# Output projection: the recurrent half ahead of the memory attention, and the attentions traced later

## The chip, the cores and the metric

One Trainium2 chip, one of its cores. The kernel is one launch of one layer of a decoder trunk, batch 1, 256 tokens, model width 1024, all in float32. The metric is the device time in microseconds (us) of that launch. The layer's weights (about 84 MB) are read from HBM once.

## What is computed

```
x = x + 0.5 * swiglu(rms_norm(x, ffn1_norm), ffn1_w_in, ffn1_w_out)
u = rms_norm(x, mix_norm) @ w_in                     # 1024 -> 2048 columns
lru_x, lru_g, mq, mk, mv, cq = split(u)              # 512, 512, 256, 256, 256, 256
y_lru  = rg_lru(causal_conv4(lru_x)) * gelu(lru_g)   # recurrent half, 512 columns
y_moba = causal self-attention(mq, mk, mv)           # 4 heads x 64, ALiBi, QK norm
y_mem  = attention(cq, keys and values of rms_norm(mem) @ mem_w_kv)   # 4 heads x 64
x = x + concat(y_lru, y_moba, y_mem) @ w_out         # rows 0:512, 512:768, 768:1024
x = x + 0.5 * swiglu(rms_norm(x, ffn2_norm), ffn2_w_in, ffn2_w_out)
```

With 256 tokens there is one block of 256, so the block selection of the self-attention reduces to causal attention.

## The kernel before

**Products.** Every weight is split into a high part (`whi`) and a low part (`wlo`), every activation too, and a product is three TensorE (PE) matmuls: high times high, low weight times high, high weight times low. One such matmul has 128 rows and 512 columns. Tokens come in two tiles, t = 0 and 1.

**The stream.** All weights form one list, `stream`, of steps. A step is one half of a 1 MB unit: `halve` makes `whi` on ScalarE (ACT, line 119) and `wlo` on VectorE (DVE, line 121), three steps ahead, and `consume` traces the products of the step, 12 matmuls. Units are loaded by DMAs that SP issues, up to three units ahead (`raw`, 3 buffers); the halves have 7 buffers. Counted from `marks["kv"]`, steps 0 to 3 are the memory's keys and values, 4 to 7 the recurrent input (`use_x`), 8 to 11 queries and keys of the self-attention (`use_qk`), 12 to 15 its values and the memory's queries (`use_vc`), 16 to 19 the gate branch with its GeLU (`use_g`), 20 to 27 the output projection, and from 28 on the second FFN.

**Work beside the products.** `at(name, fn)` traces a piece of the mixer when the stream has come to step `PLAN[name]`. The pieces are the recurrence (`lru0` to `lru5`, lines 538 to 577), the transposes of the normed heads (`qkT`, `cT`; line 460, copied out of PSUM in lines 463 and 465), the scores of the self-attention (`moba_s`, line 606, softmax in 581 to 597), the scores of the memory attention (`mem_s`, line 619), the two `attend` (`moba_y`, `mem_y`; transposes of the probabilities in line 633, copies `pT` in lines 636 to 639, values in line 643, normed rows turned in line 652, split into parts in lines 150 and 151), and the turn of the recurrent output (`out0`, `out1`, line 704). The order of the trace is what the scheduler starts from; the order it settles on is fixed per engine, and each engine takes its instructions one after another.

**PSUM.** `ps_h` has 2 buffers (the products `h`), `ps_t` 2 (transposes), `ps_o` 4 (FFN outputs, gate products, scores, `y` of both attentions, and the four accumulators `o` of the projection).

**Heads' norm.** `heads_T` squares on ACT (line 449), sums on DVE (451), takes the power on GpSimd (POOL, lines 156 and 157), scales on DVE (454). The scaled rows `hsq` are what line 460 transposes.

**Projection.** `out_att` takes `yb` (self-attention) at steps 20 and 21 and `yc` (memory attention) at steps 22 and 23. `out_lru` holds four halves and at step 27 multiplies `ya` (recurrent half) by all four, tile by tile, adds the residual and transposes for the second FFN.

Of the kernel before, what the change touches and what calls it, by code (L numbers as in the profile page):

```python
# [8 lines left out]
F32 = mybir.dt.float32  # L9
# [6 lines left out]
P = 128  # L16
# [7 lines left out]
HD = 64  # L24
# [10 lines left out]
# steps after the memory's product at which the mixer's parts are traced  # L35
PLAN = dict(mk0=7, mkT0=7, mk1=6, mkT1=5, lxT0=8, lxT1=9, conv0=8, conv1=8, conv2=9, conv3=9, gate_a=10, gate_x=10,
            lru0=13, lru1=14, lru2=15, lru3=15, lru4=18, lru5=19, qkT0=11, qkT1=11, moba_s0=11, moba_s1=11, moba_y=17,
            cT0=15, cT1=15, mem_s0=15, mem_s1=15, mem_y=17, out0=21, out1=21)
WIDE = (0, 0, 0, 0, 0)
ORDER = (0, 2, 1, 3)  # heads in the order of the score tiles: two heads of one row tile share a PSUM bank  # L40
# [5 lines left out]
def hymba_layer(ctx, tc, x, mem, ffn1_norm, ffn1_w_in, ffn1_w_out, mix_norm, mem_norm, w_in,  # L46
# [22 lines left out]
    @contextmanager  # L69
    def in_order():  # L70
        """Each engine takes what is traced here in the order of the trace."""
        traced = nc.cur_bb.bb.instructions
        at = len(traced)
        yield
        last = {}
        for i in traced[at:]:
            if i.engine in last:
                tc.add_manual_dep(i, last[i.engine], mybir.DependencyInfo(
                    mybir.DependencyClass.NoSync, mybir.DependencyReason.DATA), reason="in_order")
            last[i.engine] = i.name  # L80

# [16 lines left out]
    class Unit:  # L98
# [3 lines left out]
        def load(self, part=None):  # L102
            """loads(raw): the DMAs' (tile, DRAM rows), in the order of the k tiles."""
# [8 lines left out]
        def halve(self, i, ways=1, pool_ways=()):  # L112
            """The i-th half's high and low parts, in steps: yields after each of the ways."""
# [16 lines left out]
    def in_unit(w, c0s, width, k0, single=False):  # L130
        """Four k tiles of w's columns [c0, c0 + width) for the given c0s: [P, 4, 512]."""
# [11 lines left out]
    def out_unit(w, r0):  # L143
        """Two k tiles of whole rows: [P, 2, 1024]."""
        wv = w[0, r0:r0 + 2 * P, :].rearrange("(k p) n -> p k n", p=P)
        return Unit(2, lambda raw: [(raw.rearrange("p (k n) -> p k n", k=2), wv)])

# [5 lines left out]
    def rsqrt(ss, n, count, out):  # L153
        """out = (ss / count + eps) ** -0.5, [P, n], on GpSimd."""
# [4 lines left out]
    def row_scale(a, name):  # L159
        """rsqrt(mean(a * a) + eps) over the row, [P, 1]."""  # L160
# [7 lines left out]
    def transposed(a, g, t, pre, src_pool=None):  # L168
        """(a * g) with the features on partitions, in two float32r parts."""
        return finish(transposed_steps(a, g, t, pre, src_pool))  # L170

    def transposed_steps(a, g, t, pre, src_pool=None):
        """Each half's transposes, scalings, high parts and low parts: yields after each of the eight."""
# [24 lines left out]
    stream = []  # L198

    def project(units, xT, use, wide=False):  # L200
        """h[t] = x[t] @ the two units' columns; then use(t, h)."""
# [128 lines left out]
    def later(fn, *args):  # L330
        """Traces fn's instructions behind all that was traced so far on each engine."""
# [6 lines left out]
    def parameters():  # L338
# [39 lines left out]
        # softplus(-lam) = max(-lam, 0) + 2 atanh(e / (2 + e)), e = exp(-|lam|)  # L378
# [26 lines left out]
        # ALiBi and the causal mask: the block on the diagonal, and the one below it  # L405
# [38 lines left out]
    def heads_T(name, src, n, dsts):  # L444
        """src [P tokens, n * HD]: RMS norm over each head, then dims on partitions."""
# [92 lines left out]
    def rate():  # L538
        """2 sigmoid(z) = exp(min(z, 0)) * (1 + |tanh(z / 2)|), right to the last bits for small ones too."""
# [5 lines left out]
    def decay():  # L545
        """th = tanh(s / 2), a = exp(-s) = (1 - th) / (1 + th), 1 - a^2 = 4 th / (1 + th)^2."""
# [7 lines left out]
    def decay2():  # L554
        """One Newton step from (1 + exp(-s)) / 2 towards 1 / (1 + th)."""
# [25 lines left out]
    def softmax_rows(s, w, from_psum):  # L581
        """exp(s - max) / sum over the last axis: [P, NH, w], heads in the order ORDER."""
# [30 lines left out]
    def mem_scores(t):  # L613
        ss = []
        for i in range(2):
            s = ps_o.tile([P, 2, SEQ], F32, name="s", tag="o")
# [6 lines left out]
    def attend(pr, v, causal, name):  # L623
        """y transposed: [P (two heads' dims), pair, tokens], in two parts."""
        pr, v = L[pr], L[v]
        wk = L["wk"]
        ys = [ps_o.tile([P, NH, HD], F32, name="y", tag="o") for _ in range(NT)]
# [54 lines left out]
    # the GeLU branch  # L682
# [48 lines left out]
    def out_lru(k):  # L731
        def go(u):
            held.append(u)
            if k < 3:
                return
            for t in range(NT):
                x2[t] = resp.tile([P, D], F32, name=f"xd{t}", tag="res")
                for hf in range(2):
                    for i in range(4):
                        out_rows(L["ya"], i, t, (hf,), held[i], False, i == 3)  # L740
# [7 lines left out]
    for r0, fns in ((512, [out_att("yb", k, True) for k in range(2)]), (768, [out_att("yc", k, False) for k in range(2)]),  # L748
                    (0, [out_lru(0), out_lru(1)]), (256, [out_lru(2), out_lru(3)])):
# [20 lines left out]
    def load_ahead(i):  # L770
        """Loads as many units as there is room for, when the halves before i are split."""
# [80 lines left out]
```

## Time and profile before

| | |
|---|---|
| time, median of 3 runs | 502.61 us (502.40 to 502.68) |
| span of the profiled execution | 501.6 us |
| PE busy | 485.5 us, 97% of the span |
| PE weight loads busy | 396.1 us, 79% |
| DVE busy | 314.8 us, 63% |
| ACT busy | 256.5 us, 51% |
| POOL busy | 30.2 us, 6% |
| moved by DMA | 87.70 MB, 52.4% of the 16 engines' span on the main queue |
| granted TensorE clock | full, in every one of the 40 slices |

The time of a run is 1.0 us over the span of the profiled execution; the sum in the prediction is made against the span, and the 1.0 us is added at the end. Matmuls are pipelined: a row of one matmul gives 0.39 to 0.50 us, but the next starts 0.23 us later, so gaps on PE are best read from start to start. An idle time that a row prints counts from the modelled end of the matmul before, and is thus 0.16 us shorter than the time lost.

### The profile page before, as it was taken

What the parts mean: (1) busy time and instruction counts of PE and PEld (TensorE: products, weight loads), DVE (VectorE), ACT (ScalarE), POOL (GpSimd) and SP (SyncE); (2) the same over time, 40 slices, a digit from 0 to 9 for tenths busy, and PEclk for the clock granted to TensorE, in tenths of its full rate; (3) what the DMA queues carried; (4) which work ended last, traced back from release to release, by engine and by line L of the source; (5) the groups of instructions that cost most, each with busy time, mean ns of one, the idle gap of its engine ahead of it and who ended that gap; (6) DMA issues with size and microseconds to landing.
All of it is one profiled execution on the core that took longest, in us unless ns stands there. A gap on an engine that the chain in (4) does not pass through costs nothing.

```text
span 501.6 us, 5950 instructions
## 1 busy us (share of the span) xinstructions
PE 485.5 (97%) x2246; PEld 396.1 (79%) x2246; DVE 314.8 (63%) x423; ACT 256.5 (51%) x365; POOL 30.2 (6%) x53
## 2 busy tenths in 40 slices
PE   4999999999999999999889999999999999999996
PEld 4877888888888888887667887888888888888885
DVE  4886765565575648855889667865565556555532
ACT  4853544444455445755799646544444444444410
POOL 2540000000000000120320000100000000000000
PEclk9999999999999999999999999999999999999999
DMA  8985665565655556256032542855565556555202
GB/s 262 296 281 185 206 218 169 181 215 189 202 177 172 205 196 225 94 186 223 30 139 84 169 140 90 274 169 169 189 219 179 169 174 209 198 175 167 85 0 84
DMA packets 61580, 87.70 MB, mean 175 GB/s; under 512 B 3377, under 2 KB 48497, under 8 KB 61553
## 3 DMA queue, kind: packets, MB, share of 16 engines
q1 hardware_dynamic: 61552, 87.34, 52.4%
q8 instruction: 17, 0.28, 0.2%
q14 instruction: 11, 0.08, 0.1%
HBM read 86.28 MB, written 1.05 MB: 174 GB/s over the span
## 4 chain that ended last, share of the span: by engine, by line
PE 86%; DVE 6%; ACT 3%; DMA 2%; POOL 1%; issue 1%; SPq 0%; ACTq 0%
PE h L213 52%; PE o L274 24%; PE o L718 4%; DMA raw<-in_ffn_w_in 2%; PE tp L260 2%; DVE wlo L121 1%; PE tp L182 1%; ACT whi L119 1%; PE y L643 1%; POOL hr L157 1%; DVE xb L515 1%; PE tp L633 0%; ACT pr L594 0%; DVE nm L591 0%; POOL var L156 0%
## 5 line engine op out<-in xcount | busy, mean ns | idle before, releaser
L121 DVE TENSOR_TENSOR wlo<-raw,whi 128x1024 fp32r<-128x1024 f32 (+1 forms) x162 | 194.2, 1206 | 140.4 <-ACT whi L119 140.3
L119 ACT ACTIVATE whi<-raw 128x1024 fp32r<-128x1024 f32 (+1 forms) x164 | 168.6, 1038 | 169.7 <-PE h L213 98.7
L213 PE MATMUL h<-whi,ah 128*128 128x512 f32 x176 | 70.1, 400 | 2.6 <-ACT ah L190 2.6
L274 PE MATMUL o<-whi,gh 128*128 128x512 f32 x176 | 70.4, 400 | 0.7 <-DVE g L249 0.5
L213 PE MATMUL h<-wlo,ah 128*128 128x512 f32 x176 | 69.7, 396 | 0.0
L213 PE MATMUL h<-whi,ch 128*128 128x512 f32 x176 | 69.6, 396 | 0.0
L274 PE MATMUL o<-wlo,gh 128*128 128x512 f32 x176 | 69.4, 394 | 0.0
L213 PE MATMUL h<-whi,al 128*128 128x512 f32 x176 | 69.2, 393 | 0.0
L213 PE MATMUL h<-wlo,ch 128*128 128x512 f32 x176 | 68.5, 390 | 0.0
L213 PE MATMUL h<-whi,cl 128*128 128x512 f32 x176 | 68.4, 390 | 0.0
L274 PE MATMUL o<-whi,gl 128*128 128x512 f32 x176 | 56.7, 396 | 0.0
L213 PEld LDWEIGHTS h<-whi,ah 128*128 128x128 f32 x176 | 33.4, 191 | 9.6 <-ACT ah L190 3.0
L274 PEld LDWEIGHTS o<-whi,gh 128*128 128x128 f32 x176 | 33.1, 188 | 9.5 <-issue 1.6
L274 PEld LDWEIGHTS o<-whi,gl 128*128 128x128 f32 x176 | 33.1, 188 | 7.9
L213 PEld LDWEIGHTS h<-whi,al 128*128 128x128 f32 x176 | 33.5, 190 | 6.9
L274 PEld LDWEIGHTS o<-wlo,gh 128*128 128x128 f32 x176 | 33.1, 188 | 7.2
L213 PEld LDWEIGHTS h<-wlo,ah 128*128 128x128 f32 x176 | 33.5, 190 | 6.7
L213 PEld LDWEIGHTS h<-whi,cl 128*128 128x128 f32 x176 | 33.0, 188 | 6.9
L213 PEld LDWEIGHTS h<-whi,ch 128*128 128x128 f32 x176 | 33.1, 188 | 6.8 <-ACT ch L190 0.4
L245 ACT ACTIVATE th<-h,rh 128x256 f32<-128x256 f32 x44 | 20.9, 476 | 34.3 <-PE h L213 33.4
L213 PEld LDWEIGHTS h<-wlo,ch 128*128 128x128 f32 x176 | 33.1, 188 | 6.5
L213 PE MATMUL h<-whi,bh 128*128 128x512 f32 x64 | 26.1, 408 | 0.8 <-ACT vc L469 0.8
(191 smaller groups left out, 502.0 us busy)
## 6 DMA issues: line engine op xcount, KB each, us to landing
raw<-in_ffn_w_in SPq DMA_DIRECT2D x84, 512.0 KB
raw<-in_ffn_w_out SPq DMA_DIRECT2D x22, 1024.0 KB
raw<-in_w_in SPq DMA_DIRECT2D x8, 1024.0 KB
raw<-in_w_out SPq DMA_DIRECT2D x4, 1024.0 KB
raw<-in_ffn_w_in SPq DMA_DIRECT2D x8, 256.0 KB
raw<-in_mem_w_kv SPq DMA_DIRECT2D x2, 1024.0 KB
x<-in_x SPq DMA_DIRECT2D x4, 256.0 KB
mem<-in_mem SPq DMA_DIRECT2D x2, 512.0 KB
```

What stands on the lines that cost most here:

```text
L119: nc.scalar.activation(hi[:, s], raw[:, s], AF.Copy)
L121: sub(lo[:, s], raw[:, s], hi[:, s].bitcast(F32))
L157: nc.gpsimd.tensor_tensor(out, v, mhalf[:, :n], op=OP.pow)
L182: nc.tensor.transpose(p[:, k, :], a[:, (4 * b + k) * P:(4 * b + k + 1) * P], ident)
L213: mm(hs[t], lhsT=x[i][:, 2 * q + k, :], rhs=u[j][:, k, :], start=q == k == i == j == 0, stop=q == 3 and k == 1 and i == 1)
L245: nc.scalar.activation(th, h[:, :FC], AF.Tanh, scale=st["rh"][t])
L260: nc.tensor.transpose(p[:, k, t, :], st["g", c, t][:, k * P:(k + 1) * P], ident)
L274: mm(st["o"][t][hf], lhsT=g[:, k, t, :], rhs=u[j][:, 0, hf * 512:(hf + 1) * 512], start=c == k == 0 and g is gh and j == 0, stop=c == NFC ...
L515: nc.vector.scalar_tensor_tensor(xb, xc[:, c, j:j + SEQ], cw[:, j * CT + c:j * CT + c + 1], xb, op0=OP.mult, op1=OP.add)
L643: mm(ys[t][:, x, :], lhsT=pT[:, t, k, :], rhs=v[k][:, h * HD:(h + 1) * HD], start=k == 0, stop=k == n - 1)
L718: mm(L["o"][t][hf], lhsT=y[i][:, k, t * P:(t + 1) * P], rhs=u[j][:, 0, hf * 512:(hf + 1) * 512], start=first and i == j == 0, stop=last an ...
```

## The change

The projection takes its units in another order: rows of the self-attention (steps 20, 21), then the first half of the recurrent rows (22, 23, new `out_first`, each half multiplied at once), then the second half of the recurrent rows and the rows of the memory attention (24 to 27, `out_last`, held and multiplied together at step 27). Scores and `y` of the memory attention take PSUM from `ps_h` in place of `ps_o`. Ten of the pieces beside the products get later steps, four of the recurrence's six earlier ones. Work and sizes of all instructions stay the same, on every engine; comments are dropped.

```diff
-            lru0=13, lru1=14, lru2=15, lru3=15, lru4=18, lru5=19, qkT0=11, qkT1=11, moba_s0=11, moba_s1=11, moba_y=17,
-            cT0=15, cT1=15, mem_s0=15, mem_s1=15, mem_y=17, out0=21, out1=21)
+            lru0=12, lru1=13, lru2=14, lru3=15, lru4=16, lru5=18, qkT0=13, qkT1=13, moba_s0=13, moba_s1=14, moba_y=18,
+            cT0=18, cT1=18, mem_s0=19, mem_s1=20, mem_y=23, out0=21, out1=21)
...
     def mem_scores(t):
         ss = []
         for i in range(2):
-            s = ps_o.tile([P, 2, SEQ], F32, name="s", tag="o")
+            s = ps_h.tile([P, 2, SEQ], F32, name="s", tag="h")
...
-        ys = [ps_o.tile([P, NH, HD], F32, name="y", tag="o") for _ in range(NT)]
+        ys = [(ps_o if causal else ps_h).tile([P, NH, HD], F32, name="y", tag="o" if causal else "h") for _ in range(NT)]
...
-    def out_lru(k):
+    def out_first(k):
+        def go(u):
+            for t in range(NT):
+                out_rows(L["ya"], k, t, (0, 1), u, False, False)
+        return go
+
+    def out_last(k):
+
         def go(u):
             held.append(u)
             if k < 3:
                 return
+            parts = [("ya", 2), ("ya", 3), ("yc", 0), ("yc", 1)]
             for t in range(NT):
                 x2[t] = resp.tile([P, D], F32, name=f"xd{t}", tag="res")
                 for hf in range(2):
-                    for i in range(4):
-                        out_rows(L["ya"], i, t, (hf,), held[i], False, i == 3)
+                    for i, (y, n) in enumerate(parts):
+                        out_rows(L[y], n, t, (hf,), held[i], False, i == 3)
...
-    for r0, fns in ((512, [out_att("yb", k, True) for k in range(2)]), (768, [out_att("yc", k, False) for k in range(2)]),
-                    (0, [out_lru(0), out_lru(1)]), (256, [out_lru(2), out_lru(3)])):
+    for r0, fns in ((512, [out_att("yb", k, True) for k in range(2)]), (0, [out_first(0), out_first(1)]),
+                    (256, [out_last(0), out_last(1)]), (768, [out_last(2), out_last(3)])):
```

Three places show how the instructions move.

The first is ACT, behind the exponential of the recurrence's `rate` (line 541): `qT` and `kT` are the turned queries and keys that the scores read, `lth` and `ta` the recurrence's `decay`. Before:

```order
L541 ACTIVATE er<-er 128x1024
L465 ACTIVATE qT<-tp,gb 128x2x128
L463 ACTIVATE kT<-tp 128x2x128
L465 ACTIVATE qT<-tp,gb 128x2x128
L463 ACTIVATE kT<-tp 128x2x128
L542 ACTIVATE ta<-ta 128x1024
L119 ACTIVATE whi<-raw 128x1024
```

After:

```order
L541 ACTIVATE er<-er 128x1024
L542 ACTIVATE ta<-ta 128x1024
L119 ACTIVATE whi<-raw 128x1024 x2
L465 ACTIVATE qT<-tp,gb 128x2x128
L550 ACTIVATE lth<-ta,sp_494 128x256 x4
L552 ACTIVATE ta<-ta,sp_496 128x256 x4
L463 ACTIVATE kT<-tp 128x2x128
L465 ACTIVATE qT<-tp,gb 128x2x128
L463 ACTIVATE kT<-tp 128x2x128
L469 ACTIVATE vc_2279<-h,r_0_1769 128x512
```

All eight activations of `decay` now stand between the first `qT` and the first `kT`.

The second is ACT around the self-attention's `pT`, the turned probabilities: `gsq` of line 691 is the GeLU's tanh, whose input DVE makes in line 690. Before:

```order
L636 ACTIVATE pT<-tp 128x128
L637 ACTIVATE pT<-tp 128x256
L119 ACTIVATE whi<-raw 128x1024
L469 ACTIVATE lg_2531<-h,r_0_1769 128x512
L689 ACTIVATE gsq<-h,r_0_1769 128x512
L150 ACTIVATE yb<-tp 128x512
```

After:

```order
L465 ACTIVATE cT<-tp,gc 128x2x128
L636 ACTIVATE pT<-tp 128x128
L637 ACTIVATE pT<-tp 128x256
L691 ACTIVATE gsq<-gsq 128x512
L119 ACTIVATE whi<-raw 128x1024
L636 ACTIVATE pT<-tp 128x128
L637 ACTIVATE pT<-tp 128x256
```

The GeLU's tanh and a weight half now stand between the first and the second pair of `pT` copies.

The third is PE around the scores of the memory attention (line 619, 64 of the array's 128 rows). Before they stand in one block among products:

```order
L213 MATMUL h<-whi,bl_1747 128x512
L213 MATMUL h<-whi,bh_1746 128x512
L619 MATMUL s<-mkT,cT 128x256 x8
L213 MATMUL h<-wlo,bh_1746 128x512
L213 MATMUL h<-whi,bl_1747 128x512
```

After, the first tile's four stand in three pieces among values and transposes of the self-attention:

```order
L643 MATMUL y<-vc_2279,pT 128x64
L619 MATMUL s<-mkT,cT 128x256
L643 MATMUL y<-vc_2279,pT 128x64
L643 MATMUL y<-vc_2296,pT 128x64
L643 MATMUL y<-vc_2279,pT 128x64 x2
L643 MATMUL y<-vc_2296,pT 128x64
L633 MATMUL tp<-ident,pr 128x128 x3
L619 MATMUL s<-mkT,cT 128x256 x2
L643 MATMUL y<-vc_2279,pT 128x64 x2
L643 MATMUL y<-vc_2296,pT 128x64
L619 MATMUL s<-mkT,cT 128x256
L652 MATMUL tp<-ident,yn 128x128 x2
```

The second tile's four stay in one block, among the projection's products of `yb`. So the line 619 matmuls, which were one block, are four.

## Rows read from the trace of the kernel before

**Rows 1.** The page, part 1: busy us, share of the span, instructions.
```profile
PE 485.5 (97%) x2246; PEld 396.1 (79%) x2246; DVE 314.8 (63%) x423; ACT 256.5 (51%) x365; POOL 30.2 (6%) x53
```

**Rows 2.** One stretch: length, busy us (count) of PE, PEld, DVE, ACT, POOL; clock; DMA.
```profile
265.00:282.00 17.00, 16.51 (x108) 13.89 (x108) 16.06 (x24) 15.91 (x39) 0.00 (x0) 1.00 0.46 148
```

**Rows 3.** Timeline of PE: start us, length us, instruction, [idle before it <-releaser].
```profile
244.06 0.39 PE L213 MATMUL h<-whi,bh 128*128 128x512 f32 x1
244.73 0.63 PE L460 MATMUL tp<-ident,hsq 128*128 128x128 f32 x4 [0.28 <-DVE hsq L454]
...
247.24 0.63 PE L460 MATMUL tp<-ident,hsq 128*128 128x128 f32 x4 [1.41 <-DVE hsq L454]
247.62 0.48 PE L213 MATMUL h<-whi,bh 128*128 128x512 f32 x1
247.94 0.39 PE L213 MATMUL h<-wlo,bh 128*128 128x512 f32 x1
248.17 0.40 PE L213 MATMUL h<-whi,bl 128*128 128x512 f32 x1
248.50 1.68 PE L606 MATMUL s<-kT,qT 64*128 64x128 f32 x16
250.11 0.50 PE L213 MATMUL h<-whi,bh 128*128 128x512 f32 x1
...
258.65 0.50 PE L213 MATMUL h<-whi,bh 128*128 128x512 f32 x1 [0.76 <-ACT vc L469]
...
261.98 0.41 PE L460 MATMUL tp<-ident,hsq 128*128 128x128 f32 x2 [0.54 <-DVE hsq L454]
...
263.58 0.41 PE L460 MATMUL tp<-ident,hsq 128*128 128x128 f32 x2 [1.20 <-DVE hsq L454]
...
270.80 0.43 PE L643 MATMUL y<-vc,pT 128*128 128x64 f32 x2 [0.44 <-ACT pT L636]
```

**Rows 4.** Timeline of DVE, 247 to 275 us.
```profile
247.01 2.35 DVE L121 TENSOR_TENSOR wlo<-raw,whi 128x1024 fp32r<-128x1024 f32 x2
...
249.94 1.22 DVE L543 SCALAR_TENSOR_TENSOR ta<-ta,er 128x1024 f32<-128x1024 f32 x1
...
254.22 1.19 DVE L591 TENSOR_REDUCE nm<-pr 128x4 f32<-128x1024 f32 x1
...
259.58 0.74 DVE L451 TENSOR_REDUCE hss<-hsq 128x4 f32<-128x256 f32 x2
261.40 0.43 DVE L454 TENSOR_TENSOR hsq<-vc,hr 128x256 f32<-128x256 f32 x1 [1.08 <-POOL hr L157]
...
272.54 2.44 DVE L577 TENSOR_TENSOR_SCAN xc<-ta,lm 128x256 f32<-128x256 f32 x4
```

**Rows 5.** Timeline of ACT, 248 to 262 us, and the copy of yc.
```profile
248.28 0.38 ACT L463 ACTIVATE kT<-tp 128x256 f32<-128x256 f32 x1
...
252.01 0.39 ACT L594 ACTIVATE pr<-pr,nm 128x128 f32<-128x128 f32 x1
...
253.56 0.90 ACT L550 ACTIVATE lth<-ta,sp 128x256 f32<-128x256 f32 x2
254.36 1.70 ACT L552 ACTIVATE ta<-ta,sp 128x256 f32<-128x256 f32 x4
255.96 0.49 ACT L594 ACTIVATE pr<-pr,nm 128x256 f32<-128x256 f32 x1
...
257.93 1.25 ACT L469 ACTIVATE vc<-h,r 128x512 f32<-128x512 f32 x2
...
259.80 1.28 ACT L565 ACT_TABLE_LOAD   x1
261.10 1.06 ACT L565 ACTIVATE lth<-lth 128x1024 f32<-128x1024 f32 x1
...
288.75 0.60 ACT L150 ACTIVATE yc<-tp 128x512 fp32r<-128x512 f32 x1 [2.62 <-PE tp L652]
```

**Rows 6.** Timeline of PE: the last turn of the memory attention's rows.
```profile
288.33 0.38 PE L652 MATMUL tp<-ident,yn 128*128 128x128 f32 x2
```

## The prediction

> **What bounds the kernel now.** I read the page first: PE is busy for 485.5 of 501.6 us [rows 1], and both kernels give it the same 2246 matmul records. So the change can win only where PE stands still or pays for a switch, and lose only by new waits. The start and the end of the launch are untouched, as are both FFNs, which leaves the mixer between about 244 and 310 us. There the stretches come second: from 265 to 282 us DVE is busy 16.06 and ACT 15.91 of 17.0 us [rows 2]. PE is the bound overall, but in this part its helpers are as full as it is, and both take their instructions strictly in order, so a wait that is moved off PE can come back behind another queue. Third, the timeline of PE gives each wait and its releaser [rows 3]. A product starts 0.23 us after the one before (247.94 to 248.17), or 0.32 behind transposes (247.62 to 247.94). Waits counted from start to start are the printed idle plus 0.16 us.
>
> The waits of 0.4 us and more are: the turned queries and keys at 244.73 and 247.24 (0.28 and 1.41 printed, 0.44 and 1.57 lost), the product at 258.65 that needs ACT's evacuation `vc` (0.92), the turned memory queries at 261.98 and 263.58 (0.70 and 1.36), and `y` at 270.80, waiting for `pT` (0.60). Together 5.6 us. That is all that the change can win from waits.
>
> **The change part by part.** I take the new order on each engine and walk it with the durations of the rows, on the clock of the profiled execution. Up to PE's product at 244.06 and DVE's two weight halves at 247.01 both orders are equal.
>
> *Queries and keys, two steps later.* PE now runs 15 products (with the one at 244.06) before the eight transposes, to 247.5; `hsq` is there, as 247.24 shows, with 0.2 us to spare. 2.0 us are won. Behind them stand 18 products to 252.5, then the scores. They need `kT`, and on ACT all of `decay` is now ahead of it. DVE ends its two halves at 249.3 (247.01, 2.35 long, overlapping 0.08), makes `ta` in 1.22 to 250.5 [rows 4]; ACT then takes four `lth` (0.90 for two, 0.81 start to start) and four `ta` (1.60 from 254.36 to 255.96), 3.2 us, to 253.7, and `kT` in 0.38 [rows 5]. The scores start at 254.1: **a wait of 1.6 us**.
>
> *Memory queries, three steps later.* PE runs the scores (1.6 us, 248.50 to 250.11), then 24 products, 5.6 us, to 261.3. DVE reaches the first norm `hss` with the same list as before, except a fourth weight half (about 1.15) in place of a softmax maximum of 1.19 and two reciprocals, so at about 259.4 for 259.58. From there to the transpose took 2.4 us (259.58 to 261.98 on PE; GpSimd's power lies in it) [rows 3, 4]: ready at 261.8, **a wait of 0.5**. The second tile's norm follows with 18 products as cover: no wait over 0.1. Before, both tiles paid, 2.06.
>
> *The evacuation of `vc`.* ACT, at 253.7, takes three copies (about 0.9), one evacuation and square (0.93, half of 257.93 to 259.80), a weight half (1.0, the size of the root at 261.10), table load and root (2.3), the load back (1.3), then both softmaxes, 1.55 (252.01 to 253.56) and 1.97 (255.96 to 257.93), to 263.6, and only then the second `vc` (0.65) [rows 5]. PE needs it at 263.5, after two transposes and six products: **a wait of 0.8**, for 0.92 before.
>
> *`pT` behind the GeLU.* DVE, from 261.6, has four full-width instructions (4.2 in all), the second norm with GpSimd's 1.8 us in it, three scans (0.6 each), a weight half and the GeLU's 512 columns (about 0.65, half of a full-width one), to 271.9. ACT's tanh waits for that at the head of its queue, and behind it stand a weight half (1.0) and the second `pT` (0.3): 273.7. PE comes there at 272.0 after 18 products, five transposes and the mixed stretch behind them: **a wait of 1.7**, for 0.60.
>
> *The projection's start.* `yb` is used as soon as it is made. From the last turned rows to the first product a copy and the semaphores take about 1.05 us (PE 288.33; the copy at 288.75, 0.60 long) [rows 5, 6]. Before, products of the gate branch and the memory's values covered that; now two pairs of transposes do (0.4): **a wait of 0.6**, from none.
>
> Waits after: 1.6 + 0.5 + 0.8 + 1.7 + 0.6 = 5.2, for 5.6: -0.4 us.
>
> *Switches.* A product behind transposes or plain float32 matmuls costs 0.09 more [rows 3]. In the stretch from 240 to 312 us I count 22 such returns before and 18 after: -0.4. The memory's scores, one block of 64-row matmuls, become four. The like block of line 606 takes 1.94 us from the product ahead (248.17) to the one behind (250.11); less that product (0.23), four matmuls of 256 columns in two passes (0.23 each) and four of 128 (0.115 each), 0.33 is left per block [rows 3]. Three blocks more are +1.0. Their neighbours are plain float32 matmuls, for which no row exists: zero is the lower bound, 0.42 each (with the return) the upper; I take the row's own 0.33.
>
> The Trainium skill speaks against this part of the change: "TensorEngine Tiling (Array Packing)", Key Properties, says that changing the tiling mode, unlike changing the tile, drains TensorE. By that rule every one of the new blocks would pay in full, as the block of line 606 seems to: at the upper price the time below would be 503.2, at the lower 501.9.
>
> *Costed at nothing.* The order of the projection's products: same count. The DMAs: four loads of 1 MB in another order on SP's one queue, no wait of ACT or PE on them in this stretch. Held weights: four halves, as before. Memory scores and `y` in the two buffers of `ps_h`: the second tile's scores need the first's exponentials, and 12 products of `yb` (2.8 us) cover that; if not, PE waits for up to 1.8 us of softmax. `yc`, now last: its 1.05 us has two transposes and five products (1.2 us) in front, 0.15 to spare.
>
> Sum: -0.4 - 0.4 + 1.0 = +0.2 us. A bit of the thin covers (0.15 to 0.2 us at three places) will fail, +0.1. The span goes from 501.6 to 501.9, and with 1.0 us around it the time to **502.9 us**; the median now is 502.61.
>
> **Rivals.** *The helpers bind, and the order is indifferent.* DVE and ACT are full where PE waits [rows 2]; a small cost on PE then disappears in its waits, since PE arrives later where it would have stood anyway. The blocks' 1.0 us is in the stretch of the 1.7 us wait and right behind it. Then -0.4 - 0.4 + 0.4: 502.2 to 502.6. Against it: two of the three new blocks come after that wait.
>
> *The change does what it says and gains.* It moves transposes away from norms that were late, and 2.0 + 1.6 us of waits do leave. If `kT` and the second `pT` came in time, the waits of 1.6 and 1.7 us would be gone too: 499.6; with one of them gone, 501.3. Each is decided by a queue position: `decay` ahead of `kT`, the tanh ahead of `pT`. Only if DVE made `ta` before its two weight halves would the first vanish, and the order says otherwise.
>
> *Slower: the memory attention ends last.* Its `pT` copies stand on ACT behind two weight halves, which must wait until PE frees a buffer by a product of `ya`. If that product comes 1 us later than PE's turn to the transposes, the half (1.0) and a copy (0.6) are uncovered, and `yc`, with 0.15 to spare, follows: +1.3 us, 504.2. It decides from 0.3 us on. For it: thin covers everywhere in the new tail; before, 20 instructions lay between. Against it: the recurrent products are ready and stand in between.
>
> *The clock.* It stayed at its full level, 2.4 GHz, in the stretch with these waits [rows 2], with one of 1.57 us in the stretch before; 1.7 us is hardly longer. I give this nothing of its own.
>
> **How the numbers follow.** A measurement of this kernel can tell about 0.2% (1.0 us) from no change, so "same" is 501.6 to 503.6. Forecast as worked out: 0.55. Indifferent order: 0.15, also inside. Slower by the tail, or by more thin covers failing, over 503.6: 0.20. Faster, with one of the two queue waits gone, below 501.6: 0.10. Same is 0.70. The price of the blocks alone moves the time from 501.9 to 503.2; with the waits' own uncertainty of some 0.5 us, and the larger part of the slower rival, the range is 501.6 to 504.2.
>
> **What would show it.** In the profile after: the eight query and key transposes without a wait; about 1.6 us ahead of line 606, released by ACT `kT`; a wait near 0.8 for `vc`; about 1.7 ahead of line 643, released by `pT` with DVE's line 690 behind it; 0.6 ahead of the first `yb` product. The start-to-start times around the pieces of line 619 price the blocks. I am wrong if the summed waits in the mixer differ from 5.2 by over 1 us, if the pieces of line 619 cost nothing, or if PE stands at `yc`.

## The result, and the profile after

The changed kernel takes 507.72 us (median of 13 executions, 503.54 to 509.55) beside 502.40 for the kernel before (13 executions, 502.01 to 503.38) on the same chip: ratio 1.0083, 95% interval 1.0061 to 1.0104. It is slower, by more than the range allowed for (504.2 at most).

The median hides what happened. The mean granted TensorE clock of an execution tells two groups apart, and the number can't be understood without them: five executions at 0.999 take 503.5 to 504.3 us, eight at 0.987 to 0.990 take 507.6 to 509.6. So two things have to be explained: 1.6 us that every execution pays (503.97, the median of the five, for 502.40), and some 4.4 us more in most of them (508.37, the median of the eight).

The profiled execution (504.34 us, span 502.6) is one of the five. Its span is only 1.0 us over that of the kernel before (501.6), because the kernel before began its mixer 0.85 us later in its profiled execution (first product behind the gate products at 243.17 for 242.32). The 1.0 us between time and span, taken ahead of the prediction, set the median of some executions beside the span of another: in the runs that list both for one execution, the time is mostly 1.7 to 2.1 us over the span.

Its page, the busy times, the answer to [rows 1], and the clock over the 40 slices:

```profile
PE 487.1 (97%) x2246; PEld 396.0 (79%) x2246; DVE 314.6 (63%) x423; ACT 256.4 (51%) x365; POOL 31.0 (6%) x53
...
PEclk9999999999999999999999999999999999999999
```

By stretch (length, busy us and count of PE, PEld, DVE, ACT, POOL, clock, DMA), the answer to [rows 2] and two parts of it:

```profile
265.00:282.00 17.00, 14.85 (x86) 11.29 (x84) 14.52 (x22) 12.80 (x30) 1.51 (x2) 1.00 0.50 171
270.00:275.00 5.00, 3.32 (x21) 2.39 (x20) 5.00 (x6) 3.61 (x8) 0.00 (x0) 1.00 0.29 82
275.00:280.00 5.00, 4.53 (x30) 3.27 (x30) 3.63 (x8) 3.46 (x9) 0.00 (x0) 1.00 1.01 337
```

PE is busy for 14.85 of these 17 us, for 16.51 before. From 270 to 280 us it works for 7.85 of 10 us, and between 273 and 279 us what it does is small: matmuls of 64, 128 or 256 columns. The timeline of PE (start, length, instruction, idle before it and its releaser), the answer to [rows 3]:

```profile
253.33 1.77 PE L606 MATMUL s<-kT,qT 64*128 64x128 f32 x16 [1.54 <-ACT kT L463]
...
261.02 0.41 PE L460 MATMUL tp<-ident,hsq 128*128 128x128 f32 x2 [0.24 <-DVE hsq L454]
...
263.64 0.50 PE L213 MATMUL h<-whi,bh 128*128 128x512 f32 x1 [0.82 <-ACT vc L469]
...
270.90 0.40 PE L213 MATMUL h<-whi,bl 128*128 128x512 f32 x1
272.98 0.43 PE L643 MATMUL y<-vc,pT 128*128 128x64 f32 x2 [1.68 <-ACT pT L636]
273.35 0.70 PE L619 MATMUL s<-mkT,cT 64*128 64x256 f32 x2
273.97 1.33 PE L643 MATMUL y<-vc,pT 128*128 128x64 f32 x10
275.14 0.50 PE L633 MATMUL tp<-ident,pr 128*128 128x128 f32 x3
275.56 0.70 PE L619 MATMUL s<-mkT,cT 64*128 64x256 f32 x4
276.20 0.88 PE L643 MATMUL y<-vc,pT 128*128 128x64 f32 x6
277.01 0.70 PE L619 MATMUL s<-mkT,cT 64*128 64x256 f32 x2
277.64 0.44 PE L652 MATMUL tp<-ident,yn 128*128 128x128 f32 x2
...
279.20 0.51 PE L718 MATMUL o<-whi,yb 128*128 128x512 f32 x1 [0.47 <-ACT yb L150]
282.12 1.14 PE L619 MATMUL s<-mkT,cT 64*128 64x256 f32 x8
```

The five waits of the prediction are all there, with the releasers it named. Counted from start to start (less what one matmul takes) they are 1.70, 0.40, 0.99, 1.85 and 0.63, in sum 5.57 for the predicted 5.2. The eight query and key transposes pay nothing, and nobody waits for `yc`. On ACT the second pair of `pT` copies stands behind the tanh, for whose input, made in DVE's line 690, ACT waits 2.00 us:

```profile
271.19 0.63 ACT L691 ACTIVATE gsq<-gsq 128x512 f32<-128x512 f32 x1 [2.00 <-DVE gsq L690]
271.73 1.04 ACT L119 ACTIVATE whi<-raw 128x1024 fp32r<-128x1024 f32 x1
272.67 0.26 ACT L636 ACTIVATE pT<-tp 128x128 f32<-128x128 f32 x1
```

A piece of line 619 takes 0.62 us from start to start with one matmul (two records, 273.35 to 273.97) and 0.64 with two (four records, 275.56 to 276.20): in the piece of two the records start in pairs, 0.01 us apart, and run side by side, so a matmul that stands alone takes the time of two. Over the mixer, lines 606 and 619 with their ways in and out take PE 5.12 us for 3.84 before, from start to start: +1.28 for three blocks more. Of this, 0.43 is one pair's time (two records at 0.216 us each inside a block), since the first tile's four matmuls, two pairs in one block, take the time of three in pieces of one, two and one; some 0.28 is left for each block. By the Trainium skill, "TensorEngine Tiling (Array Packing)", Key Properties, a change of the tiling mode drains TensorE; the time that each of these pieces pays among plain float32 matmuls agrees with that.

### The profile page after: what moved, and what is told of

Its sections match the earlier page's. It is cut to its first block, busy times and chain, and to the rows that moved or that the text cites. A ratio compares the mean times of both kernels' runs of the same rounds, so it can differ in the third digit from the quotient of the medians.

```text
span 502.6 us, 5950 instructions
## 1 busy us (share of the span) xinstructions
PE 487.1 (97%) x2246; PEld 396.0 (79%) x2246; DVE 314.6 (63%) x423; ACT 256.4 (51%) x365; POOL 31.0 (6%) x53
## 4 chain that ended last, share of the span: by engine, by line
PE 86%; DVE 7%; DMA 2%; ACT 1%; POOL 1%; issue 1%; SPq 0%; ACTq 0%
PE h L213 51%; PE o L274 24%; PE o L718 4%; DMA raw<-in_ffn_w_in 2%; DVE wlo L121 2%; PE tp L260 2%; PE tp L182 1%; PE y L643 1%; POOL hr L157 1%; ACT whi L119 1%; DVE xb L515 1%; PE s L619 1%; DVE xc L577 0%; PE tp L633 0%; POOL var L156 0%
```

## The experiments

Where an experiment says that the order is held, a list at the kernel's end fixes the order of every engine to that of the kernel it starts from, so that only the named instructions move; without it the scheduler settles the order anew, and more than the named pieces can move. A time "beside" another stands beside the kernel before, measured together with it, and so do the ratios. There `more(nc, engine, r, n, fn, ...)` traces `fn` n times more, behind that engine's r-th instruction of the trace (None: the last one so far).

**The same kernel once more** (`e1_again`, no edit).

> The changed kernel itself, once more. Its executions so far form two groups: about 504.0 us with a mean granted TensorE clock of 0.999, and about 508.2 us with 0.987 to 0.990. Theory A (the fall belongs to this kernel and comes by chance of the moment in each execution): both groups again, the slower in about half or more of the executions, and the kernel before never. Theory B (it was that chip or that hour): one group only, or the kernel before shows it as well. If the profiled execution is one of the slower group, its clock column tells in which stretch the clock falls: theory A expects that stretch to lie in the mixer between 250 and 300 us and to last about 8 to 10 us at the lower level.

Measured: 508.16 us beside 502.66 (ratio 1.0102, interval 1.0080 to 1.0123). One execution of six at 0.999 (505.11 us), five at 0.987 to 0.990 (507.9 to 509.1). The two groups belong to the kernel. Of the 78 executions of the kernel before whose clocks are listed in this and the later experiments, none is under 0.993: 47 at 0.999 or more (median 502.0 us), 28 at 0.997 (median 503.0), three at 0.993 and 0.994 (503.3 to 504.4). So it loses a little of its clock too, now and then, but never 4 us.

**Three pieces of the recurrence later** (`e2_lru_early`).

```diff
-            lru0=12, lru1=13, lru2=14, lru3=15, lru4=16, lru5=18, ...
+            lru0=12, lru1=13, lru2=14, lru3=16, lru4=18, lru5=19, ...
```

> The changed kernel with three of the recurrence's pieces later (lru3 at 16, lru4 at 18, lru5 at 19), so that the GeLU's tanh reaches ACT before the second pair of pT copies is due. Only the wait of 1.85 us ahead of the self-attention's y goes; the waits for kT (1.70) and vc (0.99) stay. Without any fall of the clock: 1.3 us less than the changed kernel's faster group, about 502.6. Theory 1 (the clock falls because of the thin stretch from 267 to 280 us): the slower group is gone, all executions at 0.999 and near 502.6. Theory 2 (it falls because of the waits from 251 to 264 us, or of the tail behind 290 us): the two groups stay, near 502.6 and 506.8.

Measured: 502.76 us beside 502.66 (ratio 1.0000, interval 0.9989 to 1.0011), all eleven executions at 0.998 to 1.0. The wait for `pT` is gone, those for `kT`, `vc` and `yb` stay (1.54, 0.83 and 0.47 printed), and a short one (0.40 printed) is new ahead of the second memory queries. The slower group is gone, and with it most of the longer mixer (on PE from the first product behind the gate products to the first of the second FFN 67.20 us for 68.53, and 66.76 before).

**All six pieces as before** (`e3_lru_before`).

```diff
-            lru0=12, lru1=13, lru2=14, lru3=15, lru4=16, lru5=18, ...
+            lru0=13, lru1=14, lru2=15, lru3=15, lru4=18, lru5=19, ...
```

> The changed kernel with all six pieces of the recurrence at the steps that they had before. The scores no longer wait for kT behind decay, and the wait for pT is shorter; the projection's order and the four pieces of 64-row scores stay. Without a fall: about 1.2 us less than the changed kernel's faster group, 502.8. Theory 1 and theory 2 both expect the slower group to be gone, since both thin stretches are mended; the theory that the tail (the projection with the memory attention last) makes the clock fall expects the two groups to stay.

Measured: 507.02 us (ratio 1.0090, interval 1.0076 to 1.0105), all four executions at 0.993. (In the change five of the six pieces, not four, stand earlier than before: all but `lru3`.) Every theory missed: PE now waits 2.1 us for DVE's line 649 ahead of the turned rows, and 0.85 for `yb` shortly after. Its PE timeline:

```profile
271.88 1.13 PE L619 MATMUL s<-mkT,cT 64*128 64x256 f32 x4
274.95 0.77 PE L652 MATMUL tp<-ident,yn 128*128 128x128 f32 x4 [1.95 <-DVE yn L649]
276.41 0.50 PE L718 MATMUL o<-whi,yb 128*128 128x512 f32 x1 [0.69 <-ACT yb L150]
```

and its clock (the column behind POOL) right behind these two waits:

```profile
270.00:275.00 5.00, 3.05 (x19) 2.19 (x17) 5.00 (x9) 2.49 (x3) 0.00 (x0) 1.00 0.57 193
275.00:280.00 5.00, 4.31 (x12) 2.49 (x13) 3.08 (x6) 3.55 (x8) 0.00 (x0) 0.70 0.68 213
280.00:285.00 5.00, 5.00 (x18) 3.31 (x17) 2.23 (x5) 2.08 (x5) 0.00 (x0) 0.62 0.00 0
```

The fall, from 277.0 to 283.8 us, lies ahead of the tail behind 290, so the theory of the tail is out as well.

**The wait filled with useless work** (`e5_filled`, order held).

```diff
-            pT = wk.tile([P, NT, NT, P], F32, name="pT", tag="pT")
+            pT = wk.tile([P, NT, NT, P], F32, name="pT", tag="pT"); more(nc, "PE", 1193, 11 if causal and x == 2 else 0, nc.tensor.transpose, p[:, 1, 1, :], pr[1][0][:, x, P:2 * P], ident)
```

> The changed kernel with the order of every engine held as it is, and eleven 128x128 transposes more on TensorE: the last turned probabilities of the third head are written eleven times more, into the same place, between the last product and the y that waits 1.85 us for pT. At 0.107 us each they fill 1.2 us of that wait; y still starts when ACT has made pT, so nothing on the path is longer. Theory 1 (TensorE standing still there makes the clock fall): the slower group is gone, all executions near 504 us at a clock of 0.999 or more. Theory 2 (the fall comes from the earlier waits, from the tail or from the helpers' order): two groups as before, about 504 and 508.3.

Measured: 504.04 us (ratio 1.0030, interval 1.0016 to 1.0044), ten executions, all at 0.998 to 1.0. The PE timeline shows the filler and the same `y` behind it:

```profile
271.10 0.40 PE L213 MATMUL h<-whi,bl 128*128 128x512 f32 x1
271.33 1.36 PE L916 MATMUL tp<-ident,pr 128*128 128x128 f32 x11
273.17 0.43 PE L643 MATMUL y<-vc,pT 128*128 128x64 f32 x2 [0.47 <-ACT pT L636]
```

From the product at 271.10 to `y` are 2.07 us, as in the changed kernel (270.90 to 272.98: 2.08). Nothing is earlier; TensorE only no longer stands still. So without this standstill there is no fall in ten executions; the fall costs 4.1 us (508.16 to 504.04), and what is left, 1.7 us over the kernel before, is not the clock.

**The same kernel, 2 us later** (`e6_shifted`, order held).

```diff
-                            mm(hs[t], lhsT=x[i][:, 2 * q + k, :], rhs=u[j][:, k, :],
+                            more(nc, "PE", None, 9 if now[0] >= 50 and not EXTRA and q == k == i == j == t == 0 else 0, mm, hs[t], lhsT=x[i][:, 0, :], rhs=u[j][:, 0, :], start=True, stop=True); mm(hs[t], lhsT=x[i][:, 2 * q + k, :], rhs=u[j][:, k, :],
```

> The changed kernel with the order of every engine held as it is, and nine products of 0.23 us more in the first FFN (the first product of one group repeated, each overwritten by the next): everything behind comes 2.05 us later. Without a fall of the clock 506.0 us, with one 510.3. If the fall only depends on what TensorE does in the mixer and on the moment at which it does it, this kernel falls in some executions too, and with another moment it may do so in the profiled one: then the clock column shows the lower level from about 275 us on, behind the wait for pT, for about 10 us. If the fall comes elsewhere, the column shows where.

Measured: 510.38 and 512.16 us at 0.990 and 0.987, and this time the profiled execution has the fall. PE, with the start times of the same instructions as above:

```profile
272.66 0.40 PE L213 MATMUL h<-whi,bl 128*128 128x512 f32 x1
274.73 0.43 PE L643 MATMUL y<-vc,pT 128*128 128x64 f32 x2 [1.68 <-ACT pT L636]
...
275.72 1.75 PE L643 MATMUL y<-vc,pT 128*128 128x64 f32 x10
...
284.05 0.79 PE L718 MATMUL o<-whi,yb 128*128 128x512 f32 x1 [0.26 <-ACT yb L150]
...
288.23 1.14 PE L619 MATMUL s<-mkT,cT 64*128 64x256 f32 x8
```

```profile
270.00:275.00 5.00, 3.32 (x23) 2.56 (x21) 5.00 (x8) 2.98 (x10) 0.00 (x0) 1.00 0.00 0
275.00:280.00 5.00, 5.00 (x25) 3.62 (x24) 2.59 (x4) 3.34 (x8) 0.00 (x0) 0.65 0.96 304
280.00:285.00 5.00, 4.74 (x16) 3.45 (x16) 2.94 (x6) 1.73 (x6) 0.00 (x0) 0.50 0.35 119
285.00:290.00 5.00, 5.00 (x22) 3.58 (x21) 3.32 (x7) 2.60 (x6) 0.00 (x0) 0.83 0.00 0
```

The wait is the same (1.68 printed). The clock column has 0.65 for 275 to 280, 0.50 for 280 to 285 and 0.83 for 285 to 290: the lower level, 1.2 of 2.4 GHz, from about 276.5 to 286.7, that is from 1.7 us behind the end of the wait on, for some 10 us. From `y` to the second tile's line 619 the changed kernel takes 9.14 us at full clock (272.98 to 282.12), this one 13.50 (274.73 to 288.23): 4.36 us, which is the distance of the two groups (4.4). What about the moment decides in which execution it falls, the runs don't tell.

**A long wait in the kernel before** (`e8_before_wait` with 8 copies, `e12_before_wait_short` with 4; order held).

```diff
-                nc.scalar.activation(pT[:, 0, 0, :], p[:, 0, 0, :], AF.Copy)
+                nc.scalar.activation(pT[:, 0, 0, :], p[:, 0, 0, :], AF.Copy); more(nc, "Activation", 204, 8 if x == 0 else 0, nc.scalar.activation, pT[:, 0, 0, :], p[:, 0, 0, :], AF.Copy)
```

> The kernel before with its order held, and eight copies more on ACT: the first head's first pT is copied eight times more into the same place, 0.16 us each. The wait of 0.60 us ahead of y becomes about 1.9 us, as long as the one in the changed kernel, but with products of 512 columns on both sides. If a wait of that length by itself makes the clock fall: a slower group some 4 us above a faster one of about 503.9. If it takes the small matmuls that stand around the wait in the changed kernel as well: one group only, about 503.9, at a clock of 0.997 to 1.0.

> The kernel before with its order held and four more copies on ACT ahead of the second part of the first pT, in place of the eight of e8_before_wait. Those took 0.31 us each, so the wait ahead of y becomes 0.60 + 1.24 = 1.85 us, as in the changed kernel, but between products of 512 columns. If the length of a wait decides: the clock falls here too, in many executions, and the time has a group near 507. If the small matmuls around it are needed as well: one group near 503.6, at a clock of 0.997 or more.

Measured: with eight copies 506.88 us (ratio 1.0086, interval 1.0057 to 1.0114), all four executions at 0.988 to 0.995. The copies into one place took 0.31 us each, so the wait was 3.09 us, not 1.9:

```profile
271.75 0.69 PE L643 MATMUL y<-vc,pT 128*128 128x64 f32 x2 [2.93 <-ACT pT L906]
```

Here the clock fell while TensorE still stood: it was at the lower level from 271.5 to 278.3 us. With four copies the wait has the length of the changed kernel's:

```profile
271.00 0.43 PE L643 MATMUL y<-vc,pT 128*128 128x64 f32 x2 [1.67 <-ACT pT L906]
```

Behind it stands what stands behind that `y` in the kernel before, whose order is held: a product, some 2 us of small matmuls, then a row of products. From the kernel before:

```profile
271.04 0.48 PE L213 MATMUL h<-whi,bl 128*128 128x512 f32 x1
271.35 1.22 PE L643 MATMUL y<-vc,pT 128*128 128x64 f32 x10
272.41 0.83 PE L633 MATMUL tp<-ident,pr 128*128 128x128 f32 x6
273.00 0.47 PE L213 MATMUL h<-whi,bh 128*128 128x512 f32 x1
```

The time is 503.89 us (ratio 1.0026, interval 1.0009 to 1.0042), ten executions at 0.995 to 0.999: 1.2 us for the wait itself, the rest probably for short falls. None comes near 0.990. So in the kernel before, a wait of 1.84 us leaves most of the clock, and 3.1 us lose it; in the changed kernel a wait of the same 1.84 us, with some 6 us of 64-column values, transposes and 64-row scores behind it, brings the mean to 0.990 or less in 13 of 19 executions. That these small matmuls make the difference is argued from the two kernels: no run changes them alone, and in the changed kernel some stand ahead of the wait, too.

**Queries and keys alone** (`e4_qk_only`, the kernel before).

```diff
-            lru0=13, ..., qkT0=11, qkT1=11, moba_s0=11, moba_s1=11, moba_y=17,
+            lru0=13, ..., qkT0=13, qkT1=13, moba_s0=13, moba_s1=14, moba_y=17,
```

> The kernel before with one part of the change alone: queries and keys of the self-attention turned two steps later (qkT at 13, its scores at 13 and 14). The projection, the PSUM pools and the memory attention stay as before, so one block of 64-row scores. The two waits of 0.44 and 1.57 us at the turned queries and keys go, and decay stands no longer ahead of kT. Sum of the waits 3.2 us for 5.8 before: 1.3 to 2.6 us less than before, 500.0 to 501.3, with no slower group. If the fall of the clock belongs to the later traced self-attention by itself, a slower group appears about 4 us above that.

Measured: 502.75 us beside 502.66 (ratio 1.0002, interval 0.9994 to 1.0011). The waits of 0.44 and 1.57 us of [rows 3] are gone, and nothing is won: later on the first two of the same kinds of wait are longer than in [rows 3] (0.76, 0.54 there), and the third is about as long (1.20):

```profile
256.72 0.50 PE L213 MATMUL h<-whi,bh 128*128 128x512 f32 x1 [1.09 <-ACT vc L469]
260.73 0.41 PE L460 MATMUL tp<-ident,hsq 128*128 128x128 f32 x2 [1.68 <-DVE hsq L454]
266.08 0.44 PE L460 MATMUL tp<-ident,hsq 128*128 128x128 f32 x2 [1.12 <-DVE hsq L454]
```

**Two 64-row blocks fewer** (`e7_one_block` on `e2_lru_early`; `e11_filled_one_block` on `e5_filled`; order held). In PE's order of both:

```diff
 L643 MATMUL y<-vc_2279,pT 128x64
-L619 MATMUL s<-mkT,cT 128x256
 L643 MATMUL y<-vc_2279,pT 128x64
 ...
-L619 MATMUL s<-mkT,cT 128x256 x2
 ...
-L619 MATMUL s<-mkT,cT 128x256
+L619 MATMUL s<-mkT,cT 128x256 x4
```

> The kernel of e2_lru_early (three pieces of the recurrence later) with its order held, and one thing moved: the first tile's four matmuls of 64 rows (line 619), which stand in three pieces among the self-attention's values and turns, are put in one piece at the place of the last. Two blocks fewer, nothing else. If each block costs 0.50 us, as the start-to-start times of the changed kernel say, the time is 1.0 us less than e2_lru_early (502.76), 501.8. At the prediction's 0.33: 502.1. If the blocks' cost disappears in waits behind them (the helpers bind): 502.8, with the wait ahead of the first yb product longer by 1.0.

> The kernel of e5_filled (the changed kernel with its wait filled, so that the clock stays) with the first tile's four 64-row matmuls of line 619 in one piece in place of three: two blocks fewer in the very place where the changed kernel has them. If the blocks are what makes the changed kernel longer, 1.0 us less than e5_filled (504.04): 503.0. If they stand in time that TensorE would spend waiting for pT anyway, only the piece right behind the long wait counts: 503.5, or nothing, 504.0.

Measured: `e7_one_block` 502.44 us beside 502.31 (0.9997, 0.9984 to 1.0010), for 502.76 beside 502.66 with three pieces: no gain. PE waits now where the pieces stood:

```profile
273.07 0.93 PE L643 MATMUL y<-vc,pT 128*128 128x64 f32 x6 [0.43 <-ACT pT L636]
273.93 1.14 PE L619 MATMUL s<-mkT,cT 64*128 64x256 f32 x8
275.34 0.44 PE L652 MATMUL tp<-ident,yn 128*128 128x128 f32 x2 [0.27 <-DVE yn L649]
```

`e11_filled_one_block` took 504.85 us (1.0049, 1.0026 to 1.0072), and its clock was short again in three of six executions (0.993 to 0.997); the three at 0.999 and 1.0 took 503.17, 504.51 and 504.92. They spread too far to tell a gain of 0.5 to 1.0 us from none. In `e7_one_block` the 64-row matmuls take 1.00 us less than in `e2_lru_early` (4.12 for 5.12), and the waits 0.97 more: two blocks at 0.28 and the one pair's time (0.43) are that 1.00, but they stand in time in which PE would wait for the self-attention's copies and norms.

**The scores' wait taken away** (`e9_kT_first`, `e10_kT_norm_first`; from `e7_one_block`, order held). On ACT, for both (`e10_kT_norm_first` also moves two of DVE's instructions):

```diff
 L465 ACTIVATE qT<-tp,gb 128x2x128
-L550 ACTIVATE lth<-ta,sp_494 128x256 x4
-L552 ACTIVATE ta<-ta,sp_496 128x256 x4
 L463 ACTIVATE kT<-tp 128x2x128
 L465 ACTIVATE qT<-tp,gb 128x2x128
 L463 ACTIVATE kT<-tp 128x2x128
+L550 ACTIVATE lth<-ta,sp_494 128x256 x4
+L552 ACTIVATE ta<-ta,sp_496 128x256 x4
```

> The kernel of e7_one_block with one thing moved on ACT: the three copies kT, qT, kT (lines 463 and 465) stand ahead of the eight activations of decay, where ACT stands still for 1.26 us in e7_one_block (it waits for DVE's ta, line 543). The scores (line 606) no longer wait 1.71 us. If TensorE is the bound of the mixer, the time falls by that wait: 500.7 for 502.44. If the helpers bind, DVE and ACT reach the next things that TensorE needs no earlier, and the 1.7 us come back as longer waits ahead of the turned memory queries (line 460, 0.43 now) and of the product that needs the second vc (0.99 now): 502.2 to 502.4.

> The kernel of e9_kT_first with two of DVE's instructions moved as well: the first memory query's norm (line 451) and scaling (line 454) stand ahead of the softmax's additions and maxima, 2 to 3 us earlier. If TensorE is the bound: both waits ahead of line 460 and 606 gone, 500.3. If the helpers bind, the time follows the work that stands ahead of the second vc on ACT (two softmaxes behind DVE's maxima): 501.6 to 502.2, and the wait ahead of that product is about 2 us. 0.5 us or more under e7_one_block would make it faster than both kernels.

Measured: `e9_kT_first` 502.34 us beside 502.24 (0.9997, 0.9987 to 1.0007). The scores start without a wait, and the next thing that PE needs from DVE is no earlier (its wait was 0.43 us):

```profile
250.78 1.68 PE L606 MATMUL s<-kT,qT 64*128 64x128 f32 x16
...
260.10 0.66 PE L460 MATMUL tp<-ident,hsq 128*128 128x128 f32 x2 [1.97 <-DVE hsq L454]
```

Right behind that wait the clock of this execution was at the lower level, from 260.1 to 263.5 us; the seven executions at 0.998 or more take 501.99 to 502.71 us, so nothing is won without a fall either.

`e10_kT_norm_first` 502.36 us (1.0003, 0.9987 to 1.0020): that wait is gone too, and one of 2.8 us stands ahead of the product that needs `vc`; in two of ten executions, the profiled one among them, the mean clock was 0.992. In these two and in `e4_qk_only`, a wait taken from one place came back at another with no time won, as if the helpers set the sum of the waits and the order of PE's work chose only where they lie.

**Two weight halves on GpSimd** (`e13_two_on_pool` from `e7_one_block`, `e14_after_pool` from the changed kernel, `e15_before_pool` from the kernel before; order held).

```diff
-            ready.append(finish(u.halve(half)))
+            ready.append(finish(u.halve(half, 1, (0,) if len(ready) - marks.get("kv", 1000) in (17, 18) else ())))
```

> The kernel of e7_one_block with two of DVE's weight halves (line 121, the two of 1024 columns ahead of ta, line 543) on GpSimd, which stands still there for 13.6 us; one of 512 columns takes GpSimd 1.27 us at the start of the launch, so two of 1024 about 5.1 us beside the rest, and TensorE needs them over 10 us later. The order of all other work stays. If DVE's queue is what holds the mixer (helpers bind): ta is made up to 2.35 us earlier, decay follows until ACT's own two weight halves bound it, the scores' wait falls from 1.71 to about 0.4, and nothing gives it back: 501.2 for 502.44, faster than both kernels. If ACT's queue or the chain of GpSimd's power holds it: 502.2 to 502.5, with the waits moved behind line 460 or the second vc. If GpSimd slows DVE beside it: 502.5 or more.

> The changed kernel with its order held and only the same two weight halves on GpSimd in place of DVE. The scores' wait for kT falls from 1.70 to about 0.4 us if DVE's queue holds decay; the wait of 1.85 us for pT behind the tanh stays, and so should the fall of the clock in many executions: groups near 502.8 and 507. If the wait ahead of the scores had a part in the fall, the slower group is gone.

> The kernel before with its order held and the two weight halves that stand ahead of its ta on GpSimd in place of DVE. There decay is not what TensorE waits for, so less is won: 0.4 us, 501.9. If DVE's queue holds all that TensorE waits for: 1 us or more, 501.3.

Measured: 504.65 us (ratio 1.0049, interval 1.0036 to 1.0061), 509.75 (1.0155, 1.0140 to 1.0171) and 506.25 (1.0087, 1.0073 to 1.0100): all three slower than what they start from. Part of that is the clock (0.995 or 0.996 in four of five executions of the first, 0.990 to 0.997 in all of the third); of the second, the one execution at 1.0 took 506.30 us, for the 503.97 of the changed kernel. Beside GpSimd's two subtractions DVE's own instructions take longer. `e13_two_on_pool`, GpSimd and DVE:

```profile
244.43 5.18 POOL L121 TENSOR_TENSOR wlo<-raw,whi 128x1024 fp32r<-128x1024 f32 x2
...
244.50 2.87 DVE L454 TENSOR_TENSOR hsq<-qk,hr 128x512 f32<-128x512 f32 x1 [1.42 <-POOL hr L157]
247.29 3.40 DVE L543 SCALAR_TENSOR_TENSOR ta<-ta,er 128x1024 f32<-128x1024 f32 x1
```

and `e7_one_block`, DVE:

```profile
244.69 0.69 DVE L454 TENSOR_TENSOR hsq<-qk,hr 128x512 f32<-128x512 f32 x1 [1.43 <-POOL hr L157]
...
247.57 1.22 DVE L543 SCALAR_TENSOR_TENSOR ta<-ta,er 128x1024 f32<-128x1024 f32 x1
```

`ta`, which `decay` needs, is made 1.9 us later than with the halves on DVE (250.69 for 248.79), and the wait for `kT` grew to 2.25 us in `e13_two_on_pool` and `e14_after_pool`. So these three don't tell what a lighter DVE would bring. Which of DVE, ACT and GpSimd's power holds the sum of the waits stays open. No version was faster than both kernels; `e2_lru_early`, `e7_one_block`, `e9_kT_first` and `e10_kT_norm_first` equal the kernel before.

## Why the prediction was wrong

**The step that failed is the last rival, "The clock", with "I give this nothing of its own".** It compared the new wait of 1.7 us with the old one of 1.57 by length alone and found it hardly longer. In the changed kernel that wait brings the clock down: `e5_filled` has the same times, no standstill and no fall, and `e6_shifted` shows the fall 1.7 us behind the wait. Left out were 4.4 us in most executions. `e12_before_wait_short` bears out that a wait of this length in the kernel before loses little. What differs is most likely what stands behind it: 6 us of small matmuls up to 279.20, where in the kernel before products stand in between; no run shows this alone. The prediction had the pieces in hand (the third place of the order, and its own term for the wait), but did not put wait and stretch together. None of its three signs of being wrong appeared: the waits sum to 5.57 us, the pieces of line 619 cost time, and PE does not stand at `yc`. The clock was not among them.

**The forecast without the clock was 1.3 us short**: +0.3 us predicted, +1.6 measured (503.97 for 502.40). The mixer on PE is 1.78 us longer in the profiled execution (68.53 for 66.76): waits +0.22 (6.25 for 6.03, all from 0.2 us on counted alike), 64-row blocks +1.28, the rest +0.28.

- *Queries and keys, `kT` behind `decay`, `cT`, `vc`, `pT` behind the tanh, first product of `yb`*: right in place, releaser and size; 0, 1.70, 0.40, 0.99, 1.85 and 0.63 us for 0, 1.6, 0.5, 0.8, 1.7 and 0.6. The walk of the queues worked; 0.1 to 0.2 us too little on three of them, and small waits that it did not list (0.23 and 0.24 at the memory attention's `y`, for one of 0.22 before) turn the predicted -0.4 into +0.2.
- *Switches*: the three new blocks are +1.28 us for +1.0. The price of a block is near the row's own (0.28 for 0.33), and the doubt about plain float32 neighbours was unfounded; what the sum left out are 0.43 us for the matmuls that no longer run in pairs. But `e7_one_block` wins nothing by taking two blocks away from `e2_lru_early`. There the "thin covers", +0.1, are what is too small: between the self-attention's turn, copy, values, norm and turn no products are left, and the bare latencies (0.59 and 0.34 us of waits, once the blocks are away) are on the path with or without the blocks. For the changed kernel itself this is not shown, since the times of `e11_filled_one_block` spread too far.
- *The saved returns*, -0.4, were priced too high from [rows 3]. The next product does start 0.32 us behind a product that follows transposes, but that product itself starts 0.03 us behind the last transpose, where transposes start 0.11 us apart. Four transposes and the product take 0.70 us from start to start (247.24 to 247.94), for 4 times 0.11 and 0.23 (0.67). In the mean of the trace of the kernel before, a return costs 0.01 us behind transposes and 0.06 behind line 643. The returns did fall, from 22 to 17, which saves some 0.2 us; the +0.28 above has that in it and stays unassigned.
- *The helpers bind, and the order is indifferent* (0.15) was closer to the truth than the forecast in its mechanism, though not in its time: `e4_qk_only` and `e9_kT_first` take 2.0 and 1.7 us of waits away and win nothing. The changed kernel is longer even at full clock: it added a wait of 1.85 us behind the tanh, for which DVE, busy for all of 270 to 275 us, makes the input late; `e2_lru_early` removes that wait and is back at the time of before. Why this wait is not made up for elsewhere, as the others are, isn't shown.
- *The change gains* and *the memory attention ends last* did not happen; nothing waits for `yc`.

## What to carry to other kernels

Ask of each new wait on TensorE whether the clock outlives it, and what stands behind it: here a wait of under 2 us followed by small matmuls cost far more than itself, because the clock fell for about 10 us, and one profiled execution at full clock didn't show it; look at the clock of every execution. Where two helpers are full, count their work and not only TensorE's waits, since waits removed there came back at things that they deliver later. A wait that can't be removed can be filled with matmuls that are overwritten later: eleven transposes gave 4.1 us back. And price a switch from the start before it to the start well behind it, since what the next matmul gains can hide in the one before.

## What the runs showed of the hardware

- The granted clock went from 2.4 to 1.2 GHz after 1.85 us of standstill followed by small matmuls (`e6_shifted`, for 10.2 us), and after 2.1 and 0.85 us shortly after each other (`e3_lru_before`, for 6.8 us, 0.993 in all executions). It also fell at the end of a wait of 2.13 us (`e9_kT_first`, for 3.4 us) and during waits of 2.84 and 3.09 us (`e10_kT_norm_first`, `e8_before_wait`, for 6.8 us). Each time it came back while TensorE was busy at the lower level.
- Matmuls of 64 rows whose records start 0.01 us apart run side by side: a piece of two takes 0.64 us, a piece of one 0.62.
- DVE and GpSimd slow each other: beside GpSimd's two 128x1024 subtractions (5.18 us), DVE's scaling took 2.87 us for 0.69, and its `ta` 3.40 for 1.22. The Trainium skill, "SBUF — State Buffer", SBUF: two separate sides, says that the two share a pair of ports that one of them holds for a whole instruction; the trace agrees with that: the scaling ends 0.55 us behind the first subtraction (247.37, 246.82), `ta` 1.08 us behind the second (250.69, 249.61).
- Eight copies of 128x128 on ACT into the same place took 0.31 us each (2.44 for eight), while the pairs of `pT` copies into different places start 0.16 us apart.
